# A recurrence step over two head pairs and a quarter of the frames, and the low parts of weights on VectorE

## The chip, the core and the metric

One core of a Trainium2 chip runs the whole program. The metric is the device time of one execution in microseconds. Five engines run side by side, each with its instructions in a fixed order: TensorE (PE; its weight loads are listed apart as PEld), VectorE (DVE), ScalarE (ACT), GpSimd (POOL) and SyncE (SP), whose queue issues the DMAs.

## What is computed

A residual block over 1024 frames of 1024 channels: a gated sum of an RWKV-7 mixer and a causal convolution, then an MLP. All of it is in float32. What matters here is the mixer's recurrence, which has 16 heads of 64 channels and a 64x64 state each:

```python
def frame_step(S, inp):
    r_t, w_t, k_t, v_t, kk_t, a_t = inp
    sa = jnp.einsum('bhvk,bhk->bhv', S, -kk_t)
    S = (S * w_t[:, :, None, :]
         + sa[..., None] * (kk_t * a_t)[:, :, None, :]
         + v_t[..., None] * k_t[:, :, None, :])
    o_t = jnp.einsum('bhvk,bhk->bhv', S, r_t)
    return S, o_t
...
o = _wkv7_scan(rh, _heads(decay), kh, vh, kk, ah)     # 1024 frames, state carried on
...
u = glu_in[..., :D_CONV] * jax.nn.sigmoid(glu_in[..., D_CONV:])
u = lax.conv_general_dilated(u, conv_w[:, None, :], ...)   # causal depthwise conv, width 31
...
merged = gates[:, :, 0] * (a_out @ w_rwkv_proj[l]) + gates[:, :, 1] * (c_out @ w_conv_proj[l])
x = x + merged @ w_out[l]
x = x + jnp.square(jax.nn.relu(h2 @ w_ff1[l])) @ w_ff2[l]
```

## The kernel before

Channels lie on the 128 partitions, so one tile holds two heads (a head pair, p = 0 to 7; head h of the pair on partitions 64h to 64h+63), and frames lie along the free dimension, in two segments of 512.

**Large products.** A weight tile is loaded, and split into a rounded high part (`whi`, on ACT) and the rest (`wlo`); each product is then three matmuls of 128x512, high by high, high by low and low by high. `load_weight` (L211) does this for all weights of the first half of the program, and gives `wlo` to POOL and DVE in turn. `stream` (L236) hands out these products in threes; which unit comes next is taken from a list with conditions (L1096 and after): r, k and v of a head pair (`u_rkv`, L655), the two GLU halves of the convolution (`glu_units`, L1031), and the gates.

**Recurrence.** It is chunked: 64 frames are one chunk, whose work is done by small float32 matmuls. Work is cut into 16 items; item i is head pair i // 2 and segment i % 2, so 8 chunks. Five stages prepare or finish an item: `prep` (L699) makes decays, keys and probes, `front0` and `front1` (L801) transpose blocks (`pt`) and make the chunk's 128x128 products `pg`, four in the one head and then four in the other, `invert` (L846) inverts the triangular factors by way of DRAM (`lb`, `xz`) and POOL, `v_tm` (L778) transposes v, `group_norm` (L990) finishes. `chain` (L938) carries the state. One of its steps takes one chunk of one head pair, over three ticks: first `ps1` (tile `pc`, from `stv` and `pl`) is copied to `rsb` by DVE, and the output's first part goes to `po`; in the next tick `ps2` (from `rsb` and `z`) is copied to `sav` by DVE in two halves; in the third `ps3` (from `sav` and `bkt`) is joined by DVE with `stw`, the decayed old state that ACT made, into the next `stv`, and `po` gets its second part. So PE waits for DVE three times in a step, 384 times in all less those of each pair's last step.

**Order.** A hand-written planner goes tick by tick (L1138 and after); each `yield` in a stage ends what it issues in one tick. `PLAN` has the tick and the item's lead of each stage, NT = 24 ticks belong to an item. In each tick the live stages issue their instructions, `chain` first, then `large` fills up with products of `stream` until the tick's price on PE (TICK = 1800 ns by the planner's own prices) is used, and `conv_ops` adds up to two operations of the convolution on DVE (`fa`, `fb`; 46 for each of 8 channel tiles), while the price of DVE's work in the tick is under 0.75 of TICK. PE, DVE, ACT, POOL and SP keep the order in which this is written.

After the recurrence come the convolution's LayerNorm, the projections and the MLP, which the change doesn't touch except by which products are left over for them.

Of the kernel before, what the change touches and what calls it, by code (L numbers as in the profile page):

```python
# [10 lines left out]
F32 = mybir.dt.float32  # L11
# [6 lines left out]
P = 128  # L18
T = 1024
NK = 8  # L20
SEG = 512
NSEG = 2
NCH = 8
CW = 31
TICK = 1800.0
GAP = 1700.0
DSHARE = 0.75
NT = 24
W_LB = 2
W_XZ = 2  # L30
# [64 lines left out]
def tile_hybrid_block(ctx: ExitStack, tc: tile.TileContext, xT, win, wap, wcp, wop, wf1, wf2,  # L95
# [64 lines left out]
    z_d = [dtile(f"z_d{i}", [P, T]) for i in range(NK)]  # L160
    al_d = [dtile(f"al_d{i}", [P, T]) for i in range(NK)]
    bn_d = [dtile(f"bn_d{i}", [P, T]) for i in range(NK)]
# [46 lines left out]
    nload = [0]  # L209

    def load_weight(src):  # L211
# [307 lines left out]
    with ExitStack() as st:  # L519
        sp = st.enter_context(tc.tile_pool(name="sp", bufs=1))  # L520
        tp = st.enter_context(tc.tile_pool(name="tp", bufs=5))
        rp = st.enter_context(tc.tile_pool(name="rp", bufs=3))
# [63 lines left out]
        def zt(tag, name, dt=F32R):  # L586
            return [qp.tile([P, SEG], dt, tag=tag, name=f"{name}{i}") for i in range(NSEG)]

        def decay_and_a():
            sw, sa = zt("sav", "sw"), zt("sav", "sa")  # L590
            r1w, r1a = zt("stv", "r1w"), zt("stv", "r1a")
            r2w, xw, r2a = zt("bkt", "r2w"), zt("bkt", "xw", F32), []

            for tgt, src, hi, lo in ((sw, w2a2[0:64], H0, H1), (sa, w2a2[64:128], H1, H0)):
                for i in range(NSEG):
                    cs = slice(i * SEG, (i + 1) * SEG)
                    raw = qp.tile([P, SEG], F32, tag="pl", name="zraw")
                    sync.dma_start(raw[H0], src[:, cs])
                    sync.dma_start(raw[H1], src[:, cs])
                    full = qp.tile([P, SEG], F32R, tag="mr", name="zfull")  # L600
# [4 lines left out]
            def ev(s, ps):  # L605
                act.activation(xw[s][H0], ps[H0], AF.Tanh)
                act.activation(xw[s][H1], ps[H1], AF.Copy)
                r2a.append(qp.tile([P, SEG], F32R, tag="mr", name=f"r2a{s}"))
# [14 lines left out]
        def second_layer(_):  # L623
            sw, sa, r1w, r1a, r2w, r2a = ZA[0]
            for p in range(NK):
                i, cs = p // 4, slice((p % 4) * P, (p % 4 + 1) * P)
                for s in range(NSEG):
# [8 lines left out]
                    for ps, nm, dst in zip(pss, ("hw0", "ha0"), (z_d, al_d)):  # L636
                        t = qp.tile([P, SEG], F32, tag="pr", name="za")
# [3 lines left out]
                        sync.dma_start(dst[p][:, sl], t)  # L641
# [11 lines left out]
        RKV = {}  # L653

        def u_rkv(p, which):  # L655
# [3 lines left out]
            def evac(s, ps):  # L659
# [7 lines left out]
                def rest():  # L667
                    t = rp.tile([P, SEG], F32, tag=which, name=which)
# [4 lines left out]
                    RKV[which, NSEG * p + s] = t  # L673
# [5 lines left out]

        D = {}  # L680

# [17 lines left out]
        def prep(i):  # L699
            p, s = divmod(i, NSEG)  # L700
            sl = slice(s * SEG, (s + 1) * SEG)
            need("k", i)
            E = D[i] = {"q": [{}, {}]}
            k = RKV["k", i]
            sg, ta = t2k("sg"), t2k("ta")
            sync.dma_start(sg, z_d[p][:, sl])
            sync.dma_start(ta, al_d[p][:, sl])
            sq = t2k("sq")
            act.activation(sq, k, AF.Square, scale=v("kk", p))
# [5 lines left out]
            parts_lo(*hs, pool)  # L715
# [6 lines left out]
            ps = headsum(*hs)  # L722
            iw = cum
            act.activation(iw, cum, AF.Exp, scale=KAPPA)
            yield
# [5 lines left out]
            yield  # L731
# [3 lines left out]
            yield  # L735
            yield
            kk = rn
            dve.scalar_tensor_tensor(out=kk, in0=k, scalar=v("kk", p), in1=rn, op0=ALU.mult, op1=ALU.mult)
# [4 lines left out]
            act.activation(ta, ta, AF.Identity, scale=dv("hka", p), bias=dv("oka", p))  # L743
# [4 lines left out]
            need("r", i)  # L748
            r = RKV["r", i]
# [3 lines left out]
            dve.scalar_tensor_tensor(out=rkk, in0=r, scalar=v("rk", p), in1=k2, op0=ALU.mult, op1=ALU.mult)  # L753
            yield
            hs = parts(rkk)
            dve.tensor_tensor(out=bk[:, :, 1, :], in0=ch(k2), in1=ch(iw), op=ALU.mult)

            def probe(q):
                qs = slice(4 * q, 4 * q + 4)
                pr = E["q"][q]["pr"] = qp.tile([P, 4, 2, 64], F32, tag="pr", name="pr")  # L760
                dve.tensor_tensor(out=pr[:, :, 0, :], in0=ch(kk)[:, qs, :], in1=wt[:, qs, 0:64], op=ALU.mult)
                dve.tensor_tensor(out=pr[:, :, 1, :], in0=ch(r)[:, qs, :], in1=wt[:, qs, 1:65], op=ALU.mult)
# [9 lines left out]
            need("v", i)  # L772
# [73 lines left out]
        def invert(i):  # L846
# [46 lines left out]
            for _ in range(W_XZ):  # L893
                yield
# [1091 lines left out]
```

## Time and profile before

| | us |
|---|---|
| median of 3 runs | 2155.57 (2146.05 to 2156.53) |
| the profiled execution | 2136.36 |
| its span on the core | 2134.6 |
| span until the first product of `second_layer` (name `za`) | 97.7 |
| from there to the last matmul of `chain` | 1025.0 |
| from there to the end | 1011.9 |

The profile lists for each engine how long it was busy, and instructions grouped by the tiles that they write and read (out<-in, buffer numbers left out). A busy PE isn't PE at its peak: matmuls are pipelined, so a row's own duration (0.39 us for 128x512) is longer than the distance to the next start (0.23 us). The distance from start to start is therefore what one costs. A float32 matmul of the recurrence shows as two records, so x4 is two matmuls.

### The profile page before, as it was taken

The page shows a single profiled execution, that of the slowest core. Times are in us where ns is not written, and L with a number is a line of the kernel's source. Part 1 is how long each engine was busy: PE and PEld are TensorE (multiplying, and loading weights), DVE is VectorE, ACT ScalarE, POOL GpSimd, SP SyncE. Part 2 cuts the span into 40 slices and gives each one's busy share as a digit, 9 for nine tenths or more (in the row PEclk, how much of TensorE's full clock was granted, in tenths as well). Part 3 has the DMA queues.
Part 4 walks back from the last instruction along what each step waited for, and adds up shares of the span by engine and source line. Part 5 has one row for each costly group of instructions (what it writes and reads, how often), then busy time and mean ns, then how long its engine had stood idle before and what let it go on. Part 6 is the DMA issues. An engine that isn't in the chain of part 4 may idle for free.

```text
span 2134.6 us, 35368 instructions
## 1 busy us (share of the span) xinstructions
PE 2030.9 (95%) x12806; PEld 1538.7 (72%) x12806; DVE 1670.5 (78%) x2966; ACT 1086.4 (51%) x2046; POOL 667.5 (31%) x869
## 2 busy tenths in 40 slices
PE   6999999999999999999999999999999999999997
PEld 4767667677676666666667678777888887788886
DVE  8445989869868888888856697888676778999965
ACT  7564556555565565565433484557344445343423
POOL 4103433333332333433411222011122224455541
PEclk9999999999999999999999999999999999999999
DMA  5253222322222323222316336343544448454412
GB/s 183 76 190 79 55 60 68 85 70 80 76 74 65 90 64 83 74 84 74 91 58 217 133 134 203 133 142 134 174 143 153 153 162 265 144 165 144 124 45 79
DMA packets 235456, 246.91 MB, mean 116 GB/s; under 512 B 114833, under 2 KB 132753, under 8 KB 235281
## 3 DMA queue, kind: packets, MB, share of 16 engines
q1 hardware_dynamic: 235280, 244.65, 36.2%
q8 instruction: 101, 1.65, 0.3%
q14 instruction: 75, 0.61, 0.1%
HBM read 166.97 MB, written 77.61 MB: 115 GB/s over the span
## 4 chain that ended last, share of the span: by engine, by line
PE 65%; DVE 17%; issue 4%; DMA 4%; ACT 4%; POOL 3%; SPq 1%; POOLq 0%; DVEq 0%; ACTq 0%
PE g L114 37%; PE x L114 16%; DVE c L114 3%; PE pc L114 3%; PE pg L114 2%; DVE fa L114 2%; PE l L114 1%; PE pi L114 1%; PE po L114 1%; POOL xb L114 1%; POOL tmpb L114 1%; DMA xz<-scr_x 1%; PE pt L114 1%; DVE place L114 1%; ACT L114 1%
## 5 line engine op out<-in xcount | busy, mean ns | idle before, releaser
L114 POOL TENSOR_TENSOR wlo<-raw,whi 128x512 fp32r<-128x512 f32 x188 | 269.7, 1435 | 804.5 <-ACT whi L114 755.8
L114 PE MATMUL g<-hhi,whi 128*128 128x512 f32 x912 | 400.0, 439 | 0.0
L114 PE MATMUL g<-hhi,wlo 128*128 128x512 f32 x912 | 362.6, 398 | 2.1 <-POOL wlo L114 1.5
L114 PE MATMUL g<-hlo,whi 128*128 128x512 f32 x912 | 363.1, 398 | 0.0
L114 ACT ACTIVATE whi<-raw 128x512 fp32r<-128x512 f32 x328 | 205.0, 626 | 244.4 <-PE g L114 118.4
L114 PEld LDWEIGHTS g<-hhi,whi 128*128 128x128 f32 x912 | 172.6, 189 | 48.8 <-issue 1.9
L114 PE MATMUL g<-place,whi 128*128 128x512 f32 x640 | 202.4, 396 | 5.4 <-ACT place L114 3.7
L114 PEld LDWEIGHTS g<-hhi,wlo 128*128 128x128 f32 x912 | 173.3, 190 | 44.4 <-POOL wlo L114 2.4
L114 PE MATMUL x<-place,whi 128*128 128x512 f32 x624 | 195.9, 394 | 1.5 <-ACT place L114 0.9
L114 PEld LDWEIGHTS g<-hlo,whi 128*128 128x128 f32 x912 | 173.5, 190 | 27.3 <-issue 1.9
L114 PE MATMUL g<-a,whi 128*128 128x512 f32 x608 | 189.7, 393 | 2.7 <-ACT whi L114 1.4
L114 DVE TENSOR_TENSOR wlo<-raw,whi 128x512 fp32r<-128x512 f32 x140 | 100.7, 720 | 104.9 <-ACT whi L114 104.5
L114 PE MATMUL x<-a,whi 128*128 128x512 f32 x528 | 166.1, 396 | 10.7 <-DVE c L114 7.4
L114 PEld LDWEIGHTS g<-place,whi 128*128 128x128 f32 x640 | 120.4, 188 | 35.0 <-ACT place L114 4.1
L114 PEld LDWEIGHTS x<-place,whi 128*128 128x128 f32 x624 | 116.7, 188 | 30.1 <-ACT place L114 1.3
L114 PEld LDWEIGHTS g<-a,whi 128*128 128x128 f32 x608 | 113.6, 188 | 30.2 <-ACT whi L114 3.0
L114 ACT ACTIVATE stw<-stv,wc 64x64 f32<-64x64 f32 x240 | 82.5, 344 | 98.7 <-DVE stv L114 95.3
L114 POOL TENSOR_TENSOR tmpb<-lb,xb 64x15 f32<-64x15 f32 (+7 forms) x240 | 107.2, 447 | 80.4 <-DMA lb<-scr_l 64.2
L114 PE MATMUL g<-place,wlo 128*128 128x512 f32 x320 | 125.5, 392 | 0.6 <-DVE wlo L114 0.6
L114 PEld LDWEIGHTS x<-a,whi 128*128 128x128 f32 x528 | 99.0, 190 | 37.0 <-ACT whi L114 5.1
L114 PE MATMUL x<-place,wlo 128*128 128x512 f32 x312 | 122.0, 391 | 0.0
L114 PE MATMUL g<-a,wlo 128*128 128x512 f32 x304 | 119.0, 391 | 1.8 <-DVE wlo L114 1.0
(291 smaller groups left out, 4188.5 us busy)
## 6 DMA issues: line engine op xcount, KB each, us to landing
raw<-wf SPq DMA_DIRECT2D x128, 256.0 KB, 2.9
raw<-win SPq DMA_DIRECT2D x124, 256.0 KB, 3.0
f_d<-c SPq DMA_DIRECT2D x92, 256.0 KB, 2.3
fl<-f_d SPq DMA_DIRECT2D x76, 256.0 KB, 3.2
c<-f_d SPq DMA_DIRECT2D x30, 256.0 KB, 3.0
xt<-xT SPq DMA_DIRECT2D x16, 256.0 KB, 5.3
ga_d<-gt SPq DMA_DIRECT2D x16, 256.0 KB, 2.1
z_d<-za SPq DMA_DIRECT2D x16, 256.0 KB, 2.1
```

Source lines behind the costliest of these rows:

```text
L114: ins = f(*a, **k)
```

## The change

Item i becomes head pairs 2(i // 4) and 2(i // 4) + 1 with quarter i % 4 of the frames (256 frames): still 16 items of 8 chunk blocks, but now as 4 chunks of two pairs, tiles laid out as (pair, chunk, 64). A step of `chain` takes one chunk of both pairs, and six ticks where it took three: 64 steps, with a free tick behind each of the three phases. The decayed old state is no longer made by ACT and added by DVE: an extra matmul with the identity (`pc<-stv,cst`) adds the state into `ps3`, and DVE multiplies the sum by the decay (`tensor_tensor` in place of `scalar_tensor_tensor`, for both pairs at once). In `front` the eight `pg` matmuls of both heads are issued as one group in which the heads alternate, into two PSUM tiles.

r, k and v are written to DRAM by `u_rkv` and read back by quarters (`fetched`), since an item needs two pairs' worth. `prep` begins at tick -6 in place of 1 of the item's second lead, `front0`, `front1`, `v_tm` and `invert` move to other ticks, `invert` waits 4 ticks for `lb` and 9 for `xz` where it waited 2 and 2. `load_weight` gives `wlo` always to DVE, and the first `hsl` of `prep` moves from POOL to DVE. TICK becomes 1690, DVE's share 0.85, and `conv_ops` adds up to 3 operations in even ticks and 1 in odd ones. The GLU products of channel tile 0 and r, k, v of pair 1 come ahead of the first item.

```diff
-TICK = 1800.0
+TICK = 1690.0
-DSHARE = 0.75
+DSHARE = 0.85
-W_LB = 2
-W_XZ = 2
+W_LB = 4
...
             act.activation(hi, raw, AF.Copy)
-            eng = pool if nload[0] % 2 else dve
-            nload[0] += 1
-            eng.tensor_tensor(out=lo, in0=raw, in1=hi.bitcast(F32), op=ALU.subtract)
+            dve.tensor_tensor(out=lo, in0=raw, in1=hi.bitcast(F32), op=ALU.subtract)
...
-                    t = rp.tile([P, SEG], F32, tag=which, name=which)
+                    t = rp.tile([P, SEG], F32, tag="rkv", name="rkv", bufs=2)
...
-                    RKV[which, NSEG * p + s] = t
+                    sync.dma_start(rkv_d[which][p // 2][p % 2][:, s * SEG : (s + 1) * SEG], t)
+                    made.add((which, p, s))
...
+        def fetched(which, i):
+            pp, u = divmod(i, 4)
+            need(which, 2 * pp, u // 2)
+            need(which, 2 * pp + 1, u // 2)
+            t = rp.tile([P, SEG], F32, tag=which, name=which)
+            sync.dma_start(two(t), quarter(rkv_d[which], i))
+            return t
...
-            parts_lo(*hs, pool)
+            parts_lo(*hs)
...
-            for h in range(2):
-                rows = slice(64 * h, 64 * h + 64)
-                pg = mp.tile([P, 4, P], F32, tag="m", name="pg")
-                for j in range(4):
-                    pe.matmul(pg[:, j, :], bk[rows, 4 * q + j, :, :].rearrange("p a t -> p (a t)"),
+            pgs = [mp.tile([P, 4, P], F32, tag="m", name="pg") for h in range(2)]
+            for j, b in enumerate(blocks):
+                for h, rows in enumerate((H0, H1)):
+                    pe.matmul(pgs[h][:, j, :], bk[rows, b, :, :].rearrange("p a t -> p (a t)"),
                               pr[rows, j, :, :].rearrange("p a t -> p (a t)"), start=True, stop=True)
...
-            for c in range(NCH):
+            for c in range(4):
...
+                for e in pairs:
+                    for h in range(2):
+                        pe.matmul(ps1[hr[h], e], Q["pl"][:, h, 2 * e + cc, :], stv[:, h, 2 * e + cc, :],
+                                  start=True, stop=True)
+                rs = sp.tile([P, 2, 64], F32, tag="rsb", name="rsb", bufs=2)
+                dve.tensor_copy(rs, ps1)
...
-                    for h in range(2):
-                        act.activation(stw[hr[h]], Q["stv"][hr[h], h, j, :], AF.Copy,
-                                       scale=wc[hr[h], c, 0:1])
+                yield
                 yield
...
+                if not (u == 3 and c == 3):
+                    for e in pairs:
+                        for h in range(2):
+                            pe.matmul(ps3[hr[h], e], ident[:, 64 * h : 64 * h + 64], stv[:, h, 2 * e + cc, :],
+                                      start=True, stop=False)
+                            pe.matmul(ps3[hr[h], e], Q["bkt"][:, 2 * e + cc, 64 * h : 64 * h + 64],
+                                      sav[:, 2 * e + cc, 64 * h : 64 * h + 64], start=False, stop=True)
...
-                        dve.scalar_tensor_tensor(out=nstv[hr[h], h, nj, :], in0=ps3[hr[h]],
-                                                 scalar=wc[hr[h], c, 0:1], in1=stw[hr[h]],
-                                                 op0=ALU.mult, op1=ALU.add)
+                        dve.tensor_tensor(out=nstv[hr[h], h, nc_:4:2, :], in0=ps3[hr[h]],
+                                          in1=wc[hr[h], c:8:4, :].to_broadcast([64, 2, 64]), op=ALU.mult)
...
-        PLAN = [(1, 2, prep), (24, 0, group_norm), (15, 2, front0), (24, 2, front1), (35, 2, v_tm), (29, 2, invert)]
+        PLAN = [(-6, 2, prep), (24, 0, group_norm), (10, 2, front0), (12, 2, front1), (28, 2, v_tm), (18, 2, invert)]
...
-                conv_ops(2 if i < NI - 2 else 3, d0 + TICK * (DSHARE if i < NI - 2 else 1.0) - behind)
+                share = DSHARE if i < NI - 2 else 1.0
+                conv_ops(3 - 2 * (t % 2), d0 + TICK * (share + (-0.35 if t % 2 else 0.35)) - behind)
```

On PE, around one step of `chain` in the middle of the recurrence (`g` are the large products), there stood before:

```order
L114 MATMUL pg<-pr,bk 128x128 x4
L114 MATMUL pc<-stv,pl 64x64 x2
L114 MATMUL po<-pr,stv 64x64 x2
L114 MATMUL pg<-pr,bk 128x128 x4
L114 MATMUL g<-hhi,whi 128x512
L114 MATMUL g<-hlo,whi 128x512
L114 MATMUL g<-hhi,wlo 128x512
L114 MATMUL pc<-rsb,z_4555 64x64 x2
L114 MATMUL g<-hhi,whi 128x512
L114 MATMUL g<-hlo,whi 128x512
L114 MATMUL g<-hhi,wlo 128x512
```

and now, from the second phase of a step to the first of the next:

```order
L114 MATMUL g<-hlo,whi 128x512
L114 MATMUL g<-hhi,wlo 128x512
L114 MATMUL pc<-stv,cst 64x64
L114 MATMUL pc<-sav,bkt 64x64
L114 MATMUL pc<-stv,cst 64x64
L114 MATMUL pc<-sav,bkt 64x64
L114 MATMUL pc<-stv,cst 64x64
L114 MATMUL pc<-sav,bkt 64x64
L114 MATMUL pc<-stv,cst 64x64
L114 MATMUL pc<-sav,bkt 64x64
L114 MATMUL po<-mr,sav 64x64 x4
L114 MATMUL pg<-pr,bk 128x128 x8
```

A group of small matmuls has become twice as long and there are half as many, the eight `pg` stand in one group, and four identity matmuls have come in, each ahead of the matmul that adds to the same place.

On DVE, between two of the chain's first copies (`rsb`), there stood before:

```order
L114 COPY rsb<-pc 128x64
L114 TENSOR_TENSOR pr<-sq,wt 128x4x64
L114 TENSOR_TENSOR pr<-r,wt 128x4x64
L114 SCALAR_TENSOR_TENSOR fa<-u,cw,fa 128x512
L114 COPY sav<-pc 64x64 x2
L114 TENSOR_TENSOR hsl<-o,hsh 128x512
L114 TENSOR_TENSOR wlo<-raw,whi 128x512
L114 SCALAR_TENSOR_TENSOR stv<-pc,wc,stw 64x64 x2
L114 SCALAR_TENSOR_TENSOR fb<-u,cw,fb 128x512
L114 SCALAR_TENSOR_TENSOR fa<-u,cw,fa 128x512
```

and now, ahead of the chain's third operation and behind it:

```order
L114 COPY sav<-pc 64x2x64 x2
L114 TENSOR_TENSOR z_5627<-xz,pi 128x512
L114 SCALAR_TENSOR_TENSOR fb<-u,cw,fb 128x512
L114 SCALAR_TENSOR_TENSOR fa<-u,cw,fa 128x512
L114 TENSOR_TENSOR hsl<-sq,hsh 128x512
L114 SCALAR_TENSOR_TENSOR cum<-scanmask,sg 128x512
L114 TENSOR_TENSOR stv<-pc,wc 64x2x64 x2
L114 SCALAR_TENSOR_TENSOR fb<-u,cw,fb 128x512
L114 SCALAR_TENSOR_TENSOR fa<-u,cw,fa 128x512
L114 TENSOR_TENSOR u<-u 128x528
L114 TENSOR_TENSOR wlo<-raw,whi 128x512
```

The chain's operations are fewer and wider, and more other work stands between one and the next, with the convolution's operations in twos and threes.

## Rows read from the trace of the kernel before

**Rows 1.** The page: busy time of each engine over the span.

```profile
PE 2030.9 (95%) x12806; PEld 1538.7 (72%) x12806; DVE 1670.5 (78%) x2966; ACT 1086.4 (51%) x2046; POOL 667.5 (31%) x869
```

**Rows 2.** By stretch: start:end, length, busy PE PEld DVE ACT POOL, clock, DMA, GB/s.

```profile
97.70:1122.70 1025.00, 982.24 (x8309) 703.82 (x8307) 806.63 (x1697) 560.43 (x1164) 336.54 (x626) 0.99 0.28 79
1550.00:1600.00 50.00, 50.00 (x220) 40.89 (x219) 35.93 (x48) 20.11 (x36) 13.85 (x10) 1.00 0.40 143
```

**Rows 3.** PE in order of time, recurrence: start us, duration, tiles, records.

```profile
503.33 0.34 PE L114 MATMUL pc<-sav,bkt 128*64 128x64 f32 x4
503.50 0.29 PE L114 MATMUL po<-mr,sav 128*64 128x64 f32 x4
503.72 0.69 PE L114 MATMUL pz<-z,lm 32*32 32x32 f32 x32
504.34 0.49 PE L114 MATMUL g<-hhi,whi 128*128 128x512 f32 x1
...
505.94 0.34 PE L114 MATMUL pc<-stv,pl 128*64 128x64 f32 x4
506.20 0.33 PE L114 MATMUL po<-pr,stv 64*64 64x64 f32 x4
506.46 0.66 PE L114 MATMUL pt<-cst,bk 128*128 128x128 f32 x4
...
507.74 0.33 PE L114 MATMUL pc<-rsb,z 64*64 64x64 f32 x4
508.01 0.50 PE L114 MATMUL g<-hhi,whi 128*128 128x512 f32 x1
...
510.63 1.16 PE L114 MATMUL pg<-pr,bk 64*128 64x128 f32 x8
511.72 0.34 PE L114 MATMUL pc<-stv,pl 128*64 128x64 f32 x4
```

**Rows 4.** PE in order of time, elsewhere: a group of 16 small matmuls.

```profile
555.33 1.10 PE L114 MATMUL pi<-xz,lm 64*64 64x64 f32 x32
556.36 0.49 PE L114 MATMUL g<-hhi,whi 128*128 128x512 f32 x1
```

**Rows 5.** PE's waits from 97.7 to 1122.7 us: total us, times, longest.

```profile
PE pc L114 <- DVE stv L114: 13.8, 26, 1.2
...
PE pi L114 <- DMA xz<-scr_x: 7.8, 9, 1.5
```

**Rows 6.** DVE from 97.7 to 1122.7 us by group: busy us, mean ns of one.

```profile
L114 DVE SCALAR_TENSOR_TENSOR fa<-u,cws,fa 128x512 f32<-128x512 f32 x112 | 91.0, 813 | 2.0
...
L114 DVE SCALAR_TENSOR_TENSOR stv<-pc,wc,stw 64x64 f32<-64x64 f32 x240 | 67.8, 283 | 50.0 <-PE pc L114 44.3
L114 DVE COPY sav<-pc 64x64 f32<-64x64 f32 x256 | 55.9, 218 | 23.2 <-PE pc L114 20.6
L114 DVE TENSOR_TENSOR wlo<-raw,whi 128x512 fp32r<-128x512 f32 x49 | 35.0, 714 | 29.9 <-ACT whi L114 29.7
L114 DVE COPY rsb<-pc 128x64 f32<-128x64 f32 x128 | 28.7, 224 | 23.6 <-PE pc L114 20.6
...
L114 DVE TENSOR_TENSOR mr<-pg,cst 128x256 f32<-128x256 f32 x64 | 27.2, 425 | 0.9
```

**Rows 7.** DVE from 1098 to 1112 us by group, where POOL has little to do.

```profile
L114 DVE SCALAR_TENSOR_TENSOR fa<-u,cw,fa 128x512 f32<-128x512 f32 x7 | 5.2, 745 | 0.9 <-ACT fa L114 0.9
```

**Rows 8.** POOL from 97.7 to 1122.7 us by group.

```profile
L114 POOL TENSOR_TENSOR wlo<-raw,whi 128x512 fp32r<-128x512 f32 x50 | 72.8, 1456 | 400.5 <-ACT whi L114 385.0 <-PE g L114 15.4
```

**Rows 9.** ACT from 97.7 to 1122.7 us by group.

```profile
L114 ACT ACTIVATE stw<-stv,wc 64x64 f32<-64x64 f32 x240 | 82.5, 344 | 98.7 <-DVE stv L114 95.3
...
L114 ACT ACT_TABLE_LOAD x36 | 46.2, 1283 | 1.8 <-issue 1.1
```

**Rows 10.** DMA issues by line: KB each, median us to landing.

```profile
z_d<-za SPq DMA_DIRECT2D x16, 256.0 KB, 2.1
...
sg<-z_d SPq DMA_DIRECT2D x16, 256.0 KB, 4.7
```

More of the change, by code (lines that the diff above doesn't have):

```diff
@@ L892, in invert @@
             x0, z0 = xz[:, 0], xz[:, 1]
[L893 removed]
+            for _ in range(9):
                 yield
+            lm = sp.tile([P, NCH, 64], F32, tag="lm", name="lm")
+            dve.tensor_tensor(out=lm, in0=lt, in1=m16.unsqueeze(1).to_broadcast([P, NCH, 64]), op=ALU.mult)
+            yield
             ps = mm64(lm, x0)
@@ L943, in chain @@
             hr = [H0, H1]
+            pairs = range(2)
             po = op.tile([P, NCH, 64], F32, tag="o", name="po")
-            for c in range(NCH):
-                q, j = divmod(c, 4)
+            for c in range(4):
+                q, cc = divmod(c, 2)
                 Q = E["q"][q]
-                pc = chp.tile([P, 3, 64], F32, tag="c", name="pc")
+                stv, sav = Q["stv"], Q["sav"]
+                pc = chp.tile([P, 3, 2, 64], F32, tag="c", name="pc")
                 ps1, ps2, ps3 = pc[:, 0], pc[:, 1], pc[:, 2]
-                for h in range(2):
-                    pe.matmul(ps1[hr[h]], Q["pl"][:, h, j, :], Q["stv"][:, h, j, :], start=True, stop=True)
-                rs = sp.tile([P, 64], F32, tag="rsb", name="rsb", bufs=2)
-                dve.tensor_copy(rs, ps1)
-                for h in range(2):
-                    pe.matmul(po[hr[h], c, :], Q["stv"][hr[h], h, j, :], Q["pr"][hr[h], j, 1, :],
-                              start=True, stop=False)
-                last = s == NSEG - 1 and c == NCH - 1
-                if not last:
-                    stw = sp.tile([P, 64], F32, tag="stw", name="stw", bufs=2)
-                    for h in range(2):
-                        act.activation(stw[hr[h]], Q["stv"][hr[h], h, j, :], AF.Copy,
-                                       scale=wc[hr[h], c, 0:1])
@@ L963, in chain @@
+                yield
+                yield
+                for e in pairs:
+                    for h in range(2):
+                        pe.matmul(ps2[hr[h], e], z[hr[h], block(e, c), :], rs[hr[h], e], start=True, stop=True)
+                for h in range(2):
+                    dve.tensor_copy(sav[0:64, cc:4:2, 64 * h : 64 * h + 64], ps2[hr[h]])
                 yield
-                for h in range(2):
-                    pe.matmul(ps2[hr[h]], z[hr[h], c, :], rs[hr[h]], start=True, stop=True)
@@ L1023, in group_norm @@
             yield
-            dve.scalar_tensor_tensor(out=o, in0=o, scalar=v("lxg", p), in1=bn, op0=ALU.mult, op1=ALU.add)
+            for e in range(2):
+                dve.scalar_tensor_tensor(out=two(o)[:, e], in0=two(o)[:, e], scalar=v("lxg", 2 * (i // 4) + e),
+                                         in1=two(bn)[:, e], op0=ALU.mult, op1=ALU.add)
             yield
-            sync.dma_start(a_d[p][:, sl], o)
+            for e in range(2):
+                sync.dma_start(a_d[2 * (i // 4) + e][:, (i % 4) * QF : (i % 4 + 1) * QF], two(o)[:, e])
         convs = []
@@ L1129, in tile_hybrid_block @@
         za = second_layer(0)
-        for _ in range(4):
-            next(za)
+        while ("v", 1, 1) not in made:
+            next(za, None)
             large(pe.work + TICK)
+            conv_ops(2, dve.work + TICK * DSHARE)
         pe0 = pe.work
-        for i in range(-2, NI + 1):
-            if i == -2:
-                live = [(len(PLAN), za)]
+        live = [(len(PLAN), za)]
+        for i in range(-3, NI + 1):
             for t in range(NT):
-                if i == NI and t > 20:
+                if i == -3 and t < 18 or i == NI and t > 20:
                     continue
                 n += 1
+                tick[0] = n
                 d0 = dve.work
```

173 lines of the change are left out of this document (94 added, 79 removed).

## The prediction

> **What bounds the kernel now.** I read first the busy shares: PE is busy for 95% of the span, the next engine, DVE, for 78% [rows 1]. Then the stretches. The change works in the recurrence, from 97.7 to 1122.7 us; there PE is busy for 982.2 of 1025.0 us and DVE for 806.6, which is 79% [rows 2]. So PE sets the pace there, and only 42.8 us are open idling. Its longest waits are for DVE's `stv`, 13.8 us in 26 pieces of at most 1.2 us, and for the DMA of `xz`, 7.8 us [rows 5]: short pieces, no stage that stops.
>
> Since PE is nearly always at work, the question is what that work costs. In a stretch of nothing but large products 220 of them start in 50.00 us, so one costs 0.227 us [rows 2]. In the recurrence such a run between two groups of small float32 matmuls costs more than its members: the six products that start at 504.34 last until the next group at 505.94, 1.60 us where 6 x 0.227 is 1.36. So each run of large products carries about 0.23 us of its own, for the two changes of kind at its ends [rows 3]. The small groups have prices from start to start, too: of the chain's five groups, two matmuls each, `pc<-stv,pl` and `po<-pr,stv` cost 0.26, `pc<-rsb,z` 0.27, `pc<-sav,bkt` 0.17 and `po<-mr,sav` 0.22 us [rows 3]. Sixteen small ones in one group cost 1.03 us [rows 4], so beyond the first two, each costs (1.03 - 0.27) / 14 = 0.055 us. Size is cheap, and the beginning of a group is dear. This is what the change acts on.
>
> **The change, part by part.** All counts are from the order of instructions, between the first product of `second_layer` and the last matmul of `chain`.
>
> Fewer runs of large products. There are 409 runs before (2452 products, head sums among them), and 248 after (2458). 161 runs fewer x 0.225 us = 36.2 us less PE time. I take 0.225 for the 0.23 of the row, since shorter runs show a little less. It is real only if small groups do stand together; the order shows that they do.
>
> The chain in wider groups. Before, 128 steps cost 0.26 + 0.26 + 0.27 + 0.22 = 1.01 us each, and 120 of them 0.17 more: 149.7 us. Afterwards each group has two more matmuls, 0.11 us: 64 x (1.01 + 0.44) = 92.8 us, and 60 x 0.28 = 16.8 us for `pc<-sav,bkt`. To that come 240 identity matmuls, four in a step. No row has one. If they overlap like the others, four cost 0.22 us; if they run one at a time, they cost half of what `pg` costs each (eight records, so four matmuls of twice the columns, in 1.09 us), 0.14, together 0.55 [rows 3]. Their order speaks for a value between: in each head the identity matmul and its partner follow each other on the same place, and only the second of the two has the other head's first beside it. I take 0.33 us, 60 x 0.33 = 19.8 us, with 13 and 33 as ends. Sum 129.4; saved 20.3 us. The Trainium skill, page TensorE: Matmul & The Clock Gate, section Part 3: Packing small matmuls, says against this order that matmuls start and end strictly in the order in which they are issued; an estimate by it, with only every second pair of neighbours side by side, is about 0.44 in place of 0.33, 7 us more, which lies within the ends.
>
> `pg` in one group. Before, four matmuls in one head's 64 rows cost 1.09 us [rows 3], and 64 such groups 69.8 us. After, heads alternate, in 32 groups of eight. Float32 matmuls in the two halves of the array do run beside each other where they alternate: that is how 16 matmuls of 64 columns fit in 1.03 us [rows 4], while those of `pg` take 0.27 each for 128 columns. But those alternate in output partitions too, and the new `pg` use all 128 output partitions in both heads; no row shows that. So the gain lies between 0 and 64 x 1.09 - 32 x 1.15 = 33.0 us. I take 33, since the two heads keep apart in rows, and in PSUM tiles. The page TensorEngine Tiling (Array Packing) of the Trainium skill, section Key Properties, says that tiles of the array run independently, and its Gotcha 1 that row tiles need banks of their own, as they have here; by it the gain is 33, and no run here shows it yet.
>
> So PE's work shrinks by 36.2 + 20.3 + 33.0 = 89.5 us.
>
> DVE. The chain's operations go from 128 + 256 + 240 (28.7 + 55.9 + 67.8 = 152.4 us) to 64 + 128 + 120, each 64 columns wider. A column costs about 1 ns (425 ns for 256 columns against 224 for 64), so 64 x 0.291 + 128 x 0.285 + 120 x 0.35 = 97 us: 55 less [rows 6]. Added: 50 `wlo` from POOL [rows 8] at DVE's 0.714 us, 36 us [rows 6], 16 `hsl` of the same size, 11 us, and 48 operations cut in two, some 0.2 us each, 8 us. Another gain: `fa` takes 0.813 us in the stretch, and 0.745 where POOL has little to do [rows 6, 7]; POOL's 73 us of `wlo` end, and if that were all of the difference, 340 convolution operations would gain up to 20 us. DVE then has about 787 us of work in a stretch of 935: 84% in place of 79%. It is nearer to PE than before, but still below it.
>
> ACT loses 240 `stw` (82.5 us) and gains 26 table loads of 1.283 us, 33 us [rows 9], all in a stretch where it is busy for 560 of 1025 us [rows 2]. POOL only loses work. Both cost nothing, under the cover of PE. If ACT's cover were gone, it would be by a table load in front of a `whi`, 1.3 us each, 33 us at most.
>
> DMA and SP. 48 stores of r, k, v and 48 fetches are added, 24 MB in a stretch where the DMA engines are 28% busy [rows 2]. A store lands 2.1 us after issue, a fetch 4.7 [rows 10]. A store stands in SP's queue behind its DVE operation's wait, and weight loads stand behind it; they are issued two halves ahead. r, k and v of later pairs are due at least 21 ticks before their first `prep`. I cost this at nothing; the cover is that lead.
>
> PE's waits. Hand-offs from PE to DVE and back fall from 376 to 188 and each has a second tick, so the waits for `stv` ought to go; `invert` waits seven ticks longer for `xz` [rows 5]. Against that, DVE is fuller, and up to three convolution operations (2.2 us) may stand together ahead of a chain operation. I leave the waits as they are, 0, with -28 (the 13.8 and 7.8 us of the two rows, and 7 of the other 21 us of idling) and +15 (a third of the idling more) as ends.
>
> Outside the stretch the large products only change sides: 48 more before, 54 fewer behind, six more within. That sums to nothing.
>
> Sum: span 2134.6 - 89.5 = 2045.1. The profiled run is 1.8 us longer than its span: 2046.9. The median of the runs stands 19.2 us above the profiled one (2155.57 against 2136.36), and I add that: **2066 us**. Its own range, with the waits' ends and the identity's (-7, +13): 2031 to 2094.
>
> **The rivals.** (1) The alternating `pg` do not overlap. For: no row has this form. Against: the alternating pattern of rows 4. 33 us stay: 2099. This is also the case in which that part doesn't do what it says.
>
> (2) The waits melt. For: each hand-off has twice the time. Against: DVE's fuller queue. 2066 - 28 = 2038.
>
> (3) Slower: DVE's queue takes the pace. The place is the chain's three hand-offs. A chain operation that comes behind convolution operations makes the next chain matmul wait on PE, and all large products behind it in PE's order. If each of the 188 hand-offs had one uncovered `fa` or `fb` ahead, that would be 188 x 0.75 = 141 us, so 2207. It decides from 89.5 / 188 = 0.48 us a hand-off. For: `wlo` and `hsl` have moved to DVE, and the order shows more operations between one chain operation and the next. Against: 84% is not full, and DVE has two ticks of about 2 us (1025 us over some 457 ticks) for each hand-off.
>
> (4) The way through DRAM shows. A stage that waits for store and fetch loses 2.1 + 4.7 = 6.8 us; once for each of the 12 items behind the first two pairs, 82 us: 2148. Against: the lead of 21 ticks.
>
> **How the numbers follow.** What a measurement of this kernel can tell from no change is about 0.5%, so 2144.8 to 2166.3 is the same. Forecast 0.59, (1) 0.14, (2) 0.15, (3) 0.08, (4) 0.04. Faster is the forecast, (1) and (2): 0.88; same is (4): 0.04; slower is (3): 0.08. The range goes from the low end, 2031, to 2121: rival (1) with the identity's upper end and a part of the waits, 2099 + 13 + 9. It leaves out (3), (4) and the tails of the others, some 0.2.
>
> **What would show it.** Right: in the profile after, the distance from a run of large products to the next small group as before, `pg` groups of 16 records at about 1.15 us from start to start, the chain's third group at 0.5 to 0.7 us, and a recurrence that ends near 1045 us with PE still at 95% or more. Rival (1) shows as `pg` groups of 2.2 us; (2) as waits for `stv`, `sav` and `xz` under 5 us; (3) as PE waits for `stv`, `sav`, `rsb` and `wlo` of over 100 us, with DVE above 90% in the recurrence; (4) as waits for the fetched `k`, `r` and `v`, in `prep` or `v_tm`. The forecast falls if PE's price for small groups doesn't follow the rows, that is if a group of eight records costs twice one of four.

## The result and the profile after

The changed kernel takes 2118.43 us (median of 4 runs, 2116.75 to 2124.16), the kernel before 2155.07 (4 runs): a ratio of the means (the profiled execution before among them) of 0.986, interval 0.983 to 0.988. It is faster, but only by 37 us between the medians, where 89 were forecast. That it lies inside the range of 2031 to 2121 us is luck: the upper part of the range stood for `pg` matmuls that don't overlap, and these do overlap, as shown below. The profiled execution is one of 2117.38 us with a span of 2115.6. Between the two profiled executions the span falls by 19 us, and ends 70.5 us above the 2045.1 of the sum; between medians the shortfall is 52 us (2118.43 against 2066), since the forecast added the 19 us by which the profiled execution before was faster than its median, and the one after is only 1 us faster than its own. What follows is read from the profiled executions and accounts for the 70 us.

The page after shows the busy time of each engine, and the granted clock in 40 slices (answers to [rows 1]):

```profile
PE 1980.9 (94%) x13286; PEld 1550.2 (73%) x13286; DVE 1623.5 (77%) x2788; ACT 1044.4 (49%) x1864; POOL 508.1 (24%) x775
...
PEclk9999999999989899998999999999999999999999
```

By stretch (start:end, length, busy PE, PEld, DVE, ACT, POOL, clock, DMA share, GB/s), first until `za`, then the recurrence, then what is behind it (answers to [rows 2]):

```profile
0.00:108.50 108.50, 89.30 (x343) 67.26 (x344) 70.67 (x137) 60.24 (x99) 18.53 (x24) 0.95 0.44 141
108.50:1115.70 1007.20, 934.85 (x8795) 717.34 (x8793) 750.93 (x1491) 518.22 (x983) 206.12 (x549) 0.94 0.36 105
1115.70:2115.60 999.90, 956.71 (x4157) 765.61 (x4153) 801.92 (x1161) 465.96 (x783) 283.45 (x202) 0.99 0.46 151
```

The first stretch grew from 97.7 to 108.5 us and the last fell from 1011.9 to 999.9: the products that changed sides, which cancel as forecast. The recurrence went from 1025.0 to 1007.2 us, where 1025.0 - 89.5, with six more products (1.4 us), made 936.9. The whole miss of 70 us lies there, and its row splits it in two. PE stands idle (a stand, in what follows, is such a pause) for 1007.2 - 934.9 = 72.4 us in place of 42.8, which is 29.6 more. And PE is busy for 934.9 us, where the sum has 982.2 - 89.5 + 1.4 = 894.1, which is 40.7 more. The mean clock is 0.94 in place of 0.99: added up from the granted clock, 122.9 us of the recurrence run at 1.2 GHz, against 17.1 before.

PE in order of time shows both the prices and the stand (start us, duration, tiles, records, idle time before; answers to [rows 3, 4]):

```profile
486.04 1.16 PE L114 MATMUL pg<-pr,bk 64*128 64x128 f32 x16
487.13 0.49 PE L114 MATMUL g<-hhi,whi 128*128 128x512 f32 x1
...
488.71 0.34 PE L114 MATMUL pc<-stv,cst 128*64 128x64 f32 x4
488.88 0.29 PE L114 MATMUL pc<-sav,bkt 128*64 128x64 f32 x4
489.00 0.34 PE L114 MATMUL pc<-stv,cst 128*64 128x64 f32 x4
489.11 0.34 PE L114 MATMUL pc<-sav,bkt 128*64 128x64 f32 x4
489.23 0.45 PE L114 MATMUL po<-mr,sav 128*64 128x64 f32 x8
489.61 1.16 PE L114 MATMUL pg<-pr,bk 64*128 64x128 f32 x16
490.92 0.45 PE L114 MATMUL pc<-stv,pl 128*64 128x64 f32 x8
491.30 0.45 PE L114 MATMUL po<-pr,stv 64*64 64x64 f32 x8
495.10 1.97 PE L114 MATMUL pi<-xz,lm 64*64 64x64 f32 x32 [3.35 <-issue]
497.00 0.79 PE L114 MATMUL g<-hhi,whi 128*128 128x512 f32 x1
497.59 0.63 PE L114 MATMUL g<-hlo,whi 128*128 128x512 f32 x1
498.02 0.63 PE L114 MATMUL g<-hhi,wlo 128*128 128x512 f32 x1
```

Eight `pg` matmuls cost 1.09 us, from 486.04 to 487.13. From 488.71 to 489.23 the chain's third group takes 0.52 us with its identity matmuls. No large product stands between the second `pg` and `pi`; PE stands for 3.35 us ahead of `pi`. What follows is slow: large products start 0.43 us apart, and the `pi` group takes 1.9 us where it took 1.03 [rows 4]. The windows of this place say why (columns as above):

```profile
480.00:492.00 12.00, 11.60 (x127) 8.95 (x125) 8.93 (x20) 7.06 (x14) 0.11 (x1) 1.00 0.35 107
...
494.00:504.00 10.00, 8.90 (x103) 6.97 (x105) 4.74 (x11) 2.54 (x5) 1.93 (x8) 0.51 0.31 74
...
506.00:530.00 24.00, 24.00 (x208) 18.10 (x201) 22.41 (x44) 16.35 (x34) 11.25 (x24) 1.00 0.23 61
```

Full clock (2.4 GHz) ahead of the stand, 1.2 GHz from its last microsecond on for some 10 us, then full clock again. In the chain's part of the recurrence (from 305 us on) there are 13 such falls, about one per item, 116 us together. Eight follow a stand of 1.2 to 3.4 us ahead of `pi`. The other five, 58 us of the 116, follow a stand of 1.3 to 2.1 us ahead of `pg`, which waits for `mr`; in four of these `pi` stands again while the clock is low. The Trainium skill, page TensorE: Matmul & The Clock Gate, section HAM oscillation — how this bites in real kernels, tells of a loop in which a PE stand in every turn brings the clock down anew each time; the 13 falls agree with that pattern.

PE's waits in the recurrence (total us, times, longest; answers to [rows 5]):

```profile
PE pi L114 <- issue: 25.2, 14, 3.4
PE pg L114 <- DVE mr L114: 15.2, 17, 2.1
PE px L114 <- ACT lm L114: 7.6, 11, 0.7
PE l L114 <- ACT gsq L114: 5.9, 9, 1.4
...
PE pc L114 <- DVE stv L114: 3.5, 3, 2.1
```

The wait for `stv` has gone from 13.8 to 3.5 us. The first four rows are new or nearly so: before, `pg` and `l` had no such wait, and `px` waited for ACT for 0.3 us. The longest is that of `pi`, and it is no longer for `xz`: those DMAs were issued 20 us earlier. "issue" means that no releaser shows; the profile gave two candidates, the last operand `lm` and the PSUM bank. DVE in order of time, over the same stand:

```profile
491.21 0.75 DVE L114 SCALAR_TENSOR_TENSOR fa<-u,cw,fa 128x512 f32<-128x512 f32 x1 [0.44 <-issue]
491.88 0.75 DVE L114 SCALAR_TENSOR_TENSOR fb<-u,cw,fb 128x512 f32<-128x512 f32 x1
492.65 0.43 DVE L114 TENSOR_TENSOR pl<-pg,cst 64x256 f32<-64x256 f32 x1
493.10 0.42 DVE L114 TENSOR_TENSOR mr<-pg,cst 128x256 f32<-128x256 f32 x1
493.53 0.43 DVE L114 TENSOR_TENSOR pl<-pg,cst 64x256 f32<-64x256 f32 x1
493.97 0.42 DVE L114 TENSOR_TENSOR mr<-pg,cst 128x256 f32<-128x256 f32 x1
494.31 0.68 DVE L114 TENSOR_TENSOR lm<-lt,cst 128x512 f32<-128x512 f32 x1
```

`lm` ends at 494.99 and `pi` starts at 495.10. `lm` waits only for its turn: ahead of it stand two convolution operations and the four that empty `front1`'s two `pg` tiles, and `pi`'s own PSUM tile comes from the same two buffers of the pool `mp` as `pg`. The change itself brought them together: `invert` makes `lm` one tick ahead of `pi`, where before it was made in `invert`'s second tick, and `front1` now has its `pg` at that place.

DVE by group (busy us, mean ns of one | idle before; answers to [rows 6]):

```profile
L114 DVE SCALAR_TENSOR_TENSOR fa<-u,cws,fa 128x512 f32<-128x512 f32 x112 | 84.1, 750 | 2.8
L114 DVE TENSOR_TENSOR wlo<-raw,whi 128x512 fp32r<-128x512 f32 x100 | 69.4, 694 | 74.1 <-ACT whi L114 72.0 <-PE za L114 1.8
...
L114 DVE TENSOR_TENSOR stv<-pc,wc 64x128 f32<-64x128 f32 x120 | 34.3, 286 | 17.0 <-PE pc L114 15.6
```

`fa` fell from 813 to 750 ns, and the doubled `stv` takes 286 ns where 350 were forecast. DVE's work is 750.9 us, not 787: it has not become the bound.

### The profile page after: what moved, and what is told of

The parts are those of the page before. It is cut to its first block, busy times and chain, and to the rows that moved or that the text cites. A ratio compares the mean times of both kernels' runs of the same rounds, so it can differ in the third digit from the quotient of the medians.

```text
span 2115.6 us, 35996 instructions
## 1 busy us (share of the span) xinstructions
PE 1980.9 (94%) x13286; PEld 1550.2 (73%) x13286; DVE 1623.5 (77%) x2788; ACT 1044.4 (49%) x1864; POOL 508.1 (24%) x775
## 4 chain that ended last, share of the span: by engine, by line
PE 44%; DVE 11%; ACT 4%; issue 3%; DMA 2%; POOL 1%; DVEq 0%; POOLq 0%; ACTq 0%; SPq 0%
PE g L114 24%; PE x L114 15%; DVE c L114 3%; PE pc L114 1%; DVE place L114 1%; PE pi L114 1%; DVE fa L114 1%; ACT L114 1%; DVE wlo L114 1%; DVE a L114 1%; DMA raw<-wf 1%; PE l L114 1%; DMA fl<-f_d 1%; PE po L114 1%; ACT whi L114 1%
## 5 line engine op out<-in xcount | busy, mean ns | idle before, releaser
L114 PE MATMUL g<-hhi,whi 128*128 128x512 f32 x912 | 388.3, 426 | 3.3 <-ACT whi L114 3.3
L114 PE MATMUL g<-hlo,whi 128*128 128x512 f32 x912 | 368.4, 404 | 0.0
L114 PE MATMUL g<-hhi,wlo 128*128 128x512 f32 x912 | 368.3, 404 | 0.0
L114 DVE TENSOR_TENSOR wlo<-raw,whi 128x512 fp32r<-128x512 f32 x210 | 148.0, 705 | 148.0 <-ACT whi L114 145.6
L114 POOL TENSOR_TENSOR wlo<-raw,whi 128x512 fp32r<-128x512 f32 x118 | 169.7, 1439 | 299.8 <-ACT whi L114 263.0
L114 POOL TENSOR_TENSOR tmpb<-lb,xb 64x15 f32<-64x15 f32 (+7 forms) x240 | 88.6, 369 | 296.9 <-DMA lb<-scr_l 280.8
L114 DVE TENSOR_TENSOR c<-c,g 128x512 f32<-128x512 f32 (+1 forms) x131 | 84.9, 650 | 40.0 <-PE g L114 39.8
```

Of the source, the lines that this page charges most:

```text
L114: ins = f(*a, **k)
```

## The experiments

Three theories stood against each other for the 70 us. Theory A: `lm` comes late and `pi` shares PSUM with `pg`, so PE stands, and the clock falls. Theory B: the clock falls because small groups stand together with few large products, whether PE waits or not. Theory C: the low parts and the convolution make DVE too full. Each ratio is to the kernel before on the same chip, with its 95% interval: e1 to e4 ran on one chip, the changed kernel once more with e5 to e7 on a second, e8 to e11 on a third. Times at 1.2 GHz are of the recurrence, where nothing else is said.

> The changed kernel as it is, on the same chip as the next three, so that they can be set beside it: 0.986 of the kernel before, half-clock time in the recurrence about 116 us, one wait ahead of pi in each item.

The changed kernel again: 2114.09 us, ratio 0.986 (0.983 to 0.990), 109 us at 1.2 GHz in the chain's part, `pi` waiting for 26.5 us. The stands belong to the kernel, not to one run.

**e1: `lm` four ticks earlier, and `pi` into a bank of the pool that head sums use.**

```diff
-            for _ in range(9):
+            for _ in range(5):
                 yield
             lm = sp.tile([P, NCH, 64], F32, tag="lm", name="lm")
             dve.tensor_tensor(out=lm, in0=lt, ...)
-            yield
-            ps = mm64(lm, x0)
+            for _ in range(5):
+                yield
+            ps = mm64(lm, x0, lps())
...
-        def mm64(lhs, rhs):
-            ps = mp.tile([P, NCH, 64], F32, tag="m", name="pi")
+        def mm64(lhs, rhs, bank=None):
+            ps = mp.tile([P, NCH, 64], F32, tag="m", name="pi") if bank is None else ch(bank)
```

`pi` stays at its tick (5 and 5 in place of 9 and 1), so `lm` is now made five ticks ahead of it.

> The changed kernel with TensorE's order untouched: the masked factor lm is made five ticks earlier on VectorE, and the first product of invert (pi) goes to the head sums' PSUM bank, so that it no longer waits for the banks that front1's pg holds. Theory A (a wait of some 3 us ahead of pi in each item makes the granted clock fall to half for 3 to 14 us): the waits for pi, 25 us in all, go, time at half clock in the recurrence falls from 116 us to under 30 us, and the time from 2118 us to about 2050. Theory B (the clock falls because the small matmuls of pg and pi stand together with few large ones, wait or no wait): the waits go, the half-clock time stays near 116 us, about 2095. Theory C (VectorE's fill sets the pace): its work is the same, so the time stays within 10 us of 2118.

2056.69 us, ratio 0.960 (0.957 to 0.962). PE's order is that of the changed kernel, instruction for instruction; the recurrence is 56 us shorter, and `pi` no longer shows among PE's waits. The recurrence, and PE at the place of the stand:

```profile
108.90:1060.10 951.20, 901.80 (x8795) 691.48 (x8793) 751.47 (x1491) 519.24 (x983) 224.15 (x549) 0.98 0.38 111
```

```profile
483.66 0.45 PE L114 MATMUL po<-pr,stv 64*64 64x64 f32 x8
483.94 1.10 PE L114 MATMUL l<-xz,lm 64*64 64x64 f32 x32
484.97 0.49 PE L114 MATMUL g<-hhi,whi 128*128 128x512 f32 x1
```

The same group (its tile is called `l` now) follows `po` by 0.28 us and costs 1.03. Time at 1.2 GHz fell from 122.9 to 37.6 us. Theory A holds. DVE has as much to do as in the changed kernel (751.5 us), so theory C falls; PE's small groups stand together as they did, so theory B falls too.

The rows also tell what each part was worth, since PE does the same instructions in the same order. Of the 56 us, 23.0 are less standing (49.4 us in place of 72.4), and 33.0 are less busy time (901.8 in place of 934.9): that is the price of 85.3 us at the lower clock, 0.39 us for each. Of the falls in the chain's part five are left, four of them behind a stand of `pg`; these four take 20 us, where the five in the changed kernel took 58.

**e2: the same two operations two ticks later**, `range(9)` to `range(11)`, which moves `lm` and `pi` together away from `front1`.

> The changed kernel with lm and pi and all that follows in invert two ticks later, so that two ticks of large products come between front1's pg and pi on TensorE. Theory A: VectorE is through with front1 before pi is due, no wait, half-clock time under 30 us, about 2055 us. Theory B: the clump is thinned out, so about the same. Theory C: within 10 us of 2118.

2065.10 us, ratio 0.964 (0.962 to 0.965); 31 us at 1.2 GHz.

```profile
PE pi L114 <- issue: 11.5, 8, 1.9
```

About half of the stand stays, in pieces of at most 1.9 us, where none was expected. That it still brings most of the gain shows that what stands ahead of `lm` in DVE's queue counts, and not its distance from `pi` alone. Since large products now come between `pg` and `pi` on PE as well, e2 by itself doesn't tell theory A from theory B.

**e5 and e9: the two halves of e1 apart.** e5 has the earlier `lm` with `pi` in `mp`, e9 the bank with `lm` late.

> Half of the first experiment: lm is made five ticks earlier, but pi stays in the banks that pg uses. It then still waits for the first pg bank, which VectorE frees about 1.5 us earlier than it finished lm. Theory A (length of the stand counts): the wait ahead of pi falls from 1.8 to 3.4 us each to 0.5 to 2 us; the half-clock time falls in part, to 40 to 90 us; 2075 to 2105 us on the scale where the changed kernel has 2118. If the bank had no part in it, it would equal the first experiment: 24 us at half clock, about 0.96 of the kernel before.

> The other half of the first experiment: pi goes to the head sums' bank, lm stays late; TensorE's order as in the changed kernel. Theory A: pi waits for lm as before, 2 to 3.4 us in each item, half-clock time 90 to 120 us, 0.984 to 0.988 of the kernel before. If the bank were the cause, it would equal the first experiment, 0.960.

e5: 2078.83 us, ratio 0.969 (0.966 to 0.973), recurrence 969 us, 55 us of it at 1.2 GHz. e9: 2108.64 us, ratio 0.985 (0.982 to 0.987), recurrence 998 us, 96 us at 1.2 GHz, with PE's order unchanged. Both are as expected. PE's wait at `pi`, first in e5, then in e9:

```profile
PE pi L114 <- issue: 11.1, 10, 1.9
```

```profile
PE l L114 <- DVE lm L114: 26.0, 14, 3.3
```

In e9 the releaser has a name: `lm`, 26.0 us in 14 pieces, as much as `pi` waited in the changed kernel. The bank alone frees next to nothing; once `lm` is early, the bank is the next thing that is late (11 us), and taking it away too gives e1.

**e3: of the change only the alternating `pg`, in the kernel before.**

```diff
-            for h in range(2):
-                pg = mp.tile([P, 4, P], F32, tag="m", name="pg")
-                for j in range(4):
+            pgs = [mp.tile([P, 4, P], F32, tag="m", name="pg") for h in range(2)]
+            for j in range(4):
+                for h, rows in enumerate((H0, H1)):
...
-                yield
+            yield
+            for h, rows in enumerate((H0, H1)):
+                pg = pgs[h]
```

With the alternation one `yield` goes: the results of both heads are now taken out of PSUM in one tick, where they were taken out in two.

> The kernel before with one part of the change alone: the eight pg matmuls of a front in one group, heads in turn. As forecast, 32 groups of 1.09 to 1.15 us replace 64 of 1.09, 33 us of TensorE time less: 2155 - 33 = 2122 us if no wait grows. If the pairs cost their price and waits or a lower clock eat it, the groups measure 1.1 us and the time stays above 2140.

2139.26 us, ratio 0.998 (0.997 to 1.000): next to nothing gained, though groups of eight `pg` cost 1.09 us here too. The recurrence and PE's waits in it:

```profile
97.50:1126.80 1029.30, 961.45 (x8307) 683.78 (x8307) 804.77 (x1697) 559.48 (x1164) 337.71 (x626) 0.98 0.28 79
```

```profile
PE pc L114 <- DVE sav L114: 17.1, 20, 1.8
PE pc L114 <- DVE stv L114: 13.5, 24, 1.3
PE pi L114 <- DMA xz<-scr_x: 11.6, 11, 2.1
PE pi L114 <- DVE mr L114: 7.3, 7, 1.2
```

PE is busy for 20.8 us less than in [rows 2], and idle for 25 us more; 51 us run at 1.2 GHz, in place of 17. The cheaper group is real, and PE spends what it saved on waiting and on the lower clock. Most of the new waiting is for `sav`, 17.1 us where it was 4.0.

**e6, e7 and e8: the planner's price of `pg`.** The price is 128 columns / 2.4 x 4 = 213 ns a matmul, 1.7 us for eight, which fills a tick of 1.69 us, so `large` adds nothing to it. They take 1.09 us. Halving the price puts products into those ticks.

```diff
-            n *= KP if ... else 2 if l.shape[0] <= 64 and width(l) <= 64 else 4
+            n *= KP if ... else 2 if l.shape[0] <= 64 else 4
```

> The changed kernel with one price of the planner mended: a pg matmul is priced at half, 107 ns, nearer to the 137 ns that the trace shows, so that the ticks of pg get more large products. Theory A': the stand ahead of pi comes from lean ticks, in which the planner counts 1.7 us for a pg group that takes 1.09; TensorE gets 0.7 us later to pi for each of two groups, the wait falls from about 3.4 to 2 us, half-clock time to 40 to 90 us, 2080 to 2105 us on the scale of 2118. If the planner's price has no part in it, the wait and the time stay.

> The first experiment and the mended price together. Theory A: no wait ahead of pi is left to fill, so the price moves work only: within 10 us of the first experiment, 0.957 to 0.962 of the kernel before; a little faster if the waits of pg for the evacuation of the pg before it (14 us) are filled too: 0.955.

> The kernel before with pg in one group, as in the third experiment (0.998 of the kernel before, where 33 us less TensorE time were expected), and with pg priced at half besides. Theory D: the 33 us went into waits, because the planner still counts the old price, so that the chain's hand-offs to VectorE come sooner in real time; with the price mended, large products fill these ticks again: waits for sav, stv and xz back from 42 to about 25 us, half-clock time from 44 to about 15 us, 0.983 to 0.990 of the kernel before. Theory E: VectorE at some 80% can't go faster in that order, so it stays within 0.3% of the third experiment.

e6 (the changed kernel with this price): 2076.72 us, ratio 0.969 (0.965 to 0.973), a little better than expected. `pi` still waits, for less, and only 34 us run at 1.2 GHz, where 40 to 90 were expected:

```profile
PE pi L114 <- issue: 16.4, 14, 2.3
...
PE pg L114 <- DVE mr L114: 12.0, 17, 1.9
```

e7 (e1 with this price): 2057.39 us, ratio 0.960 (0.956 to 0.965), the same as e1; its recurrence takes more products in, and what is behind it is shorter by about as much. So the lean tick matters only as long as `lm` is late.

e8 (e3 with this price): 2129.34 us, ratio 0.994 (0.993 to 0.996), where 0.983 to 0.990 was expected. In all the cheaper `pg` is now worth about 13 us in the kernel before. The waits did fall as theory D has it: `sav`, `stv` and `xz` cost 21.8 us together, 10 us run at 1.2 GHz. The rest was lost behind the recurrence:

```profile
97.30:1106.80 1009.50, 971.39 (x8433) 695.67 (x8434) 780.48 (x1673) 566.97 (x1176) 337.18 (x628) 0.99 0.29 84
1106.80:2119.90 1013.10, 945.88 (x4081) 753.67 (x4081) 811.68 (x1170) 461.23 (x776) 306.04 (x214) 0.98 0.44 147
```

```profile
PE g L114 <- DVE y L114: 24.6, 3, 23.3
```

The recurrence holds 126 large products more than before, 28.6 us at 0.227 each; without them it would be 981 us, 44 less than before. The stretch behind has those products fewer, yet it takes 1013.1 us, as before (1011.9). PE stands there for 23.3 us in one piece, from 1153.4 to 1176.7, for `y` (the mixer's output times its gate), and the clock is at 1.2 GHz for 24 us from 1157.3 on. The loads of `y` were issued at 1172.1, in SP's queue behind a store of the convolution's `fa`, and DVE had 46 convolution operations left over for this stretch, the last until 1168.5, where the kernel before had 21. By these rows, the products that filled the ticks were missing where PE had to wait for DVE to finish the convolution.

**e4 and e11: low parts on POOL and DVE in turn**, as before the change, in the changed kernel (e4) and in e1 (e11).

```diff
-            dve.tensor_tensor(out=lo, in0=raw, in1=hi.bitcast(F32), op=ALU.subtract)
+            eng = pool if nload[0] % 2 else dve
+            nload[0] += 1
+            eng.tensor_tensor(out=lo, in0=raw, in1=hi.bitcast(F32), op=ALU.subtract)
```

> The changed kernel with one part undone: the low parts of the first half's weights go to GpSimd and VectorE by turns again. Theory A: VectorE has 36 us less of its own in the recurrence, but GpSimd's large operations slow it; the wait ahead of pi hangs on four operations of front1 and lm, not on wlo, so it stays: 2105 to 2125 us. Theory C: with VectorE's load lowered by 36 us the time falls by 20 to 35 us, to 2085 to 2098.

> The first experiment with the low parts of weights on GpSimd and VectorE by turns again. If VectorE's load counts once the stand ahead of pi is gone, 36 us less of it show as 5 to 15 us: 0.953 to 0.957 of the kernel before. If GpSimd's large operations slow VectorE by as much as they take off it, or VectorE has room, within 0.3% of 0.960.

e4: 2119.91 us, ratio 0.989 (0.988 to 0.991). e11: 2064.52 us, ratio 0.965 (0.962 to 0.967), against 0.960 for e1 on another chip; it is slower than either of its two expectations. The recurrence of e4 (columns as above) and DVE's groups there:

```profile
108.90:1114.50 1005.60, 931.50 (x8795) 713.04 (x8793) 754.71 (x1454) 518.09 (x983) 296.48 (x602) 0.95 0.36 106
```

```profile
L114 DVE SCALAR_TENSOR_TENSOR fa<-u,cws,fa 128x512 f32<-128x512 f32 x116 | 91.2, 786 | 2.7
L114 DVE TENSOR_TENSOR wlo<-raw,whi 128x512 fp32r<-128x512 f32 x49 | 34.5, 704 | 34.5 <-ACT whi L114 32.6 <-PE za L114 1.8
```

Half of `wlo`, 51 operations and 35 us, has left DVE, and DVE is busy for 754.7 us in place of 750.9. Two things fill the gap. The planner put 14 other operations in, some 10 us at 0.75 us each. And operations are slower while POOL has its share (`fa` 786 ns, not 750): the 28 us that are left, by an estimate from these rows. Sharing the low parts gains nothing here; giving them all to DVE costs nothing. Since DVE's load didn't fall, e4 and e11 don't test theory C; e1 does.

**e10: on top of e1, `front1` and `invert` one tick later** (12 to 13, and 18 to 19, in `PLAN`), meant to end the wait of `pg` for `mr`.

> The first experiment with front1 and invert one tick later, for the 14 us in which pg waits for VectorE to empty the bank of the pg before it. Theory A: that wait falls under 6 us, half-clock time in the recurrence under 15 us, 0.952 to 0.958 of the kernel before. If VectorE's fill sets that wait, it stays: 0.958 to 0.962.

2071.29 us, ratio 0.968 (0.966 to 0.970), slower than e1 and than expected. `pg` waits 10.2 us in place of 13.8, but another stage now waits:

```profile
PE pz L114 <- ACT lm L114: 14.4, 28, 1.8
```

Why ACT is late there stays open.

## Why the prediction was wrong, and where it was right

**The prices of PE's work held, in sum.** 248 runs of large products carry 0.24 us each, by the same reading that gives 0.23 over the 409 runs before. Groups of eight records cost 0.38 us where 0.33 to 0.38 were forecast. The identity matmuls cost 0.24 us a step, where I took 0.33: the group's 0.52 less 0.28 for `pc<-sav,bkt`, which is the forecast and was not measured by itself. In the rows above two identity matmuls (x4 records) start ahead of the two partners, though each partner is issued right behind its own identity matmul; so the two heads run side by side here too. The estimate of 0.44 by the Trainium skill, page TensorE: Matmul & The Clock Gate, section Part 3: Packing small matmuls, is not what the trace shows. `pg` overlaps: 1.09 us for eight in place of four, with 1.15 forecast, so rival (1) fell; the independence of tiles that the page TensorEngine Tiling (Array Packing) of the Trainium skill states in section Key Properties is now seen for this form. e1 has the changed kernel's order of work on PE and is busy for 901.8 us, with 37.6 us at 1.2 GHz. At 0.39 us for each of those, as above, it would be 893.9 at the 17.1 us of before, an estimate; the sum has 894.1. (e9, with the same order and 95.6 us at 1.2 GHz, lies on the same line: 924.6 us busy, by the line 924.3.) So the 89.5 us were there. That the terms add up this closely is in part luck: the identity matmuls and `pg` came out some 7 us cheaper than forecast, and what made up for it was not measured.

**The other terms held, but one.** DVE had 751 us of work, less than the 787 taken, so rival (3) did not come: waits for `stv`, `sav` and `rsb` are 5 us together. No wait for a fetched `r`, `k` or `v` is among PE's longest, so rival (4) fell. POOL stayed under cover, and the two outer stretches cancel. ACT, put at nothing "under the cover of PE", was less busy than before, but PE waited for it where it had not before: 7.6 us at `px`, 5.9 at `l` and 3.3 for `whi`, part of the standing below.

**The step that failed is "PE's waits. ... I leave the waits as they are, 0", with +15 us as the upper end; and the sum has no term for the clock.** I looked at the hand-offs of `chain` and at the DMA of `xz`, and for these it was right. I did not follow the operation that the change moved beside them: `lm`. It had been made many ticks ahead of its matmul; afterwards it is made one tick ahead, behind six other operations in DVE's queue at the place shown, in ticks whose price leaves them without large products. Standing grew by 29.6 us, twice the upper end that I gave, and PE's busy time came out 40.7 us above the sum, because 122.9 us ran at 1.2 GHz in place of 17.1 (105.8 us more, which at 0.39 is 41). Together these are the 70.3 us missing. e1 changes when `lm` is made and where `pi` is written, and takes away 23.0 us of the standing and 33.0 of the busy time, 56 of the 70; it lands at a ratio of 0.960, where the forecast is 2066 / 2155.57 = 0.958. So the sum of work was right, and the cost of one late operand was mis-sized at zero. The trace before had a sign of it: three of the four falls of the clock in its recurrence (13.7 of the 17.1 us) follow stands of 0.8 to 1.5 us ahead of `pi`.

**A term's gain can be absent in one kernel and present in another.** By e3 and e8 the 33 us of `pg` were worth 4 us in the kernel before, and about 13 with the price put right, when the recurrence gave them back and a stand behind it took most of that away. The sum had taken them as PE time alone.

**Open.** The recurrence of e1 is still 14.3 us longer than 936.9 (951.2): 6.6 us of standing (49.4 against 42.8) and 7.7 of busy time, for which the 20.5 us more at 1.2 GHz account by the 0.39 above. The standing has other places than before: `pg` for `mr` (13.8 us), `px` for ACT (7.7) and the head sums `l` (11.4), in place of `stv` and `xz`.

What makes the clock fall is not told in full. The length of a stand alone doesn't decide. In the changed kernel a stand of 2.07 us ahead of `pc`, at 943.4 us, with large products ahead of it and soon behind it, left the clock at 2.4 GHz, while one of 1.24 us ahead of `pi`, at 849.7, between small groups, was followed by a fall; in e3 none of the eight stands of 1.2 to 1.8 us ahead of `pc` was. Nor do the small groups by themselves: they are the same in e1. e6 keeps 16.4 us of stands ahead of `pi` with 34 us at 1.2 GHz, the changed kernel 25.2 with 123. The cause of e10's wait is open too.

e1 beats both kernels: 2056.69 us, with 2142.89 for the kernel before on the same chip; e7 is its equal.

## What to carry to other kernels

When a change moves a stage, follow every operand of its first matmul through the queue of the engine that makes it, and count what stands ahead of it there; an operand that was early for free may be late afterwards. A group that has become cheaper should become cheaper in the planner's prices as well, or its tick is left without filling work and the gain turns into waiting; and work that is drawn forward to fill it is missing later, as in e8. On a PE that is busy for 93% of a stretch, stands of 1 to 3 us among small groups cost more than their length here, 23 us of standing and 33 us of slower work: look at the granted clock of the windows behind them.

## What the hardware showed that I had not expected

- After a stand of 3.35 us, PE ran at 0.51 of its clock for some 10 us (large products 0.43 us apart, not 0.23); 13 such falls in the chain's part took 116 us at 1.2 GHz, behind stands ahead of `pi` (25 us in all) and `pg` (15 us). The same instructions took 33 us longer for 85 us more at that clock.
- Eight float32 matmuls of 64 rows and 128 output partitions take 1.09 us when the row halves alternate, and four in one half also take 1.09.
- Large POOL operations cost DVE most of what they take off it: with half of the `wlo` on POOL, 35 us, DVE's other operations took about 28 us longer, an estimate from the counts and times of e4 (754.7 us busy with 14 other operations more) and the changed kernel (750.9).
